# Encoder trunk on one core: the down product of the channel mixers by seven block products, half a part behind each gate and up unit of the next part

## The chip, the cores and the metric

The kernel runs on 1 core of one Trainium2 chip. The core has TensorE (PE, matrix products, with a separate weight load), VectorE (DVE), ScalarE (ACT), GpSimd (POOL) and SyncE (SP), which issues the DMA transfers here. Each engine works through its own queue in order and waits on semaphores of the others. The metric is the device time of one execution in microseconds (us), the median of several runs.

## What is computed

Two requests (512 and 256 tokens, 1024 features, fp32) go through two layers with the same weights. Each layer has a mixer over the sequence (a Fourier mixer first, a gated DeltaNet second) and then a channel mixer, and everything is scaled and shifted by a vector `c` (adaLN). The part that matters here is the channel mixer with its residual:

```python
def swiglu(h, w_gu, w_down):
    gu = h @ w_gu
    return (jax.nn.silu(gu[..., :FFN_DIM]) * gu[..., FFN_DIM:]) @ w_down
...
        mod = (cs @ ada_w[layer] + ada_b[layer])[:, None, :]
        sh1, sc1, g1, sh2, sc2, g2 = jnp.split(mod, 6, axis=-1)
...
        h = rmsnorm(x, norm_ffn_g[layer]) * (1.0 + sc2) + sh2
        x = x + g2 * swiglu(h, ffn_w_gu[layer], ffn_w_down[layer])
```

`FFN_DIM` is 2816, which is 22 chunks of 128.

## The kernel before

Features lie on the 128 partitions, the 768 tokens of both requests side by side in the columns. x is eight tiles `xs[m]` of 128 x 768. Every product is made in three passes: an operand is split into a rounded part (`wh`, `hh`, ...) by a cast on ACT and a remainder (`wl`, `hl`, ...) by a subtraction on DVE (`split_w`, L151 and L152, for weights; `split_to`, L199 and L200, for activations), and `passes` (L132 is the one matmul line of all helpers) adds high by high, high by low and low by high in one PSUM bank.

`gate_up` (from L375) computes gate and up of one chunk of 128 hidden features, or of two at the start. It takes the weights as a 2 x 2 block matrix (gate and up by the two halves of the inner dimension), the activations as a 2 x 2 block matrix (halves of the inner dimension by halves of the 768 tokens, `blocks`), and makes the product by seven block products (numbers 1, 2, 6, 7, 5, 4, 3, in that order) instead of eight. The weight combinations (`comb`, L379) are two on POOL and two on DVE. Below, such a pass over one chunk is called a unit; it has 7 products of 12 matmuls each.

`ffn` cuts the 22 chunks into the parts of `PARTS`. For each part it first makes all units and splits their results `sg` into `g` tiles; then, for each of the eight output rows m, `product` multiplies the part's rows of `ffn_w_down` by them, token columns 512 and 256 apart, and `residual` (L454, DVE) adds the gated result to `xs[m]`. In the second layer the last part goes to `finish`, which also normalizes and writes the output.

After each unit, and after each row of a down product, `between` advances the products of `c` with `ada_w` for later stages (`ada_steps`): fp32 matmuls that fill a quarter of PE's columns each (`sm<-at`, 4 to a step), with 256 KB transfers of their weights on SP into `AT1` = 4 buffers. This is done in the first layer alone; `AD` says how many steps go where.

The order on each engine isn't the program's text alone: the tile framework's scheduler lays the instructions of all engines out, and work marked `high_priority` (weight splits, combinations, copies out of PSUM) moves ahead. Weight tiles `wh` and `wl` have 5 buffers, fetched weights `stg` 4, `g` 10, and PSUM has 6 banks for `pr` in the first layer and 8 in the second.

Of the kernel before, what the change touches and what calls it, by code (L numbers as in the profile page):

```python
# [12 lines left out]
F32 = mybir.dt.float32  # L13
F32R = mybir.dt.float32r
AF = mybir.ActivationFunctionType
ALU = mybir.AluOpType
# [24 lines left out]
R2G = (3,)  # L41
# [68 lines left out]
def encoder_kernel(  # L110
# [264 lines left out]
    def gate_up(wgu, ms, blocks, psp, wk):  # L375

        def comb(eng, out, a, b, op):
            with tc.high_priority():
                eng.tensor_tensor(out, a, b, op)  # L379

        def parts(src):
            wh, wl = split_w(src)
            return [wh[:, k] for k in range(HK)], [wl[:, k] for k in range(HK)]

        def left(m):
            stg_g, stg_u = fetch(wgu, 0, KC, m * P), fetch(wgu, 0, KC, FFN + m * P)
            a11, a12, a21, a22 = stg_g[:, :HK], stg_g[:, HK:], stg_u[:, :HK], stg_u[:, HK:]
            yield parts(a11)
            yield parts(a12)
            s1 = wk.tile([P, HK, P], F32, name="s1", bufs=WS)  # L390
            comb(G, s1, a21, a22, ALU.add)
            comb(G, a21, a11, a21, ALU.subtract)
            comb(V, a11, s1, a11, ALU.subtract)
            yield parts(a11)
            yield parts(a21)
            yield parts(s1)
            yield parts(a22)
            comb(V, a12, a12, a11, ALU.subtract)
            yield parts(a12)

        def keep(dst, ps):
            with tc.high_priority():
                A_.copy(dst, ps[:, :HT])  # L403
# [23 lines left out]
        sg = [wk.tile([P, T], F32, name="sg", bufs=2) for _ in ms]  # L427
# [12 lines left out]

        def up2(i):
            keep(up[i][:, HT:], px[i])
            G.tensor_tensor(up[i][:, HT:], m7[i], up[i][:, HT:], ALU.add)  # L443

        step(((1, px, True, lambda i: keep(sg[i][:, :HT], px[i])), (2, pw, True, gate1)))
        step(((6, px, False, lambda i: keep(up[i][:, :HT], px[i])), (7, py, True, lambda i: keep(m7[i], py[i]))))
        step(((5, px, False, up2),
              (4, py, False, lambda i: V.tensor_tensor(up[i][:, :HT], py[i][:, :HT], up[i][:, :HT], ALU.add))))
        step(((3, px, False, gate2),))
        return sg, silu[-1]  # L450

    def residual(x, ps, gate, m):
        for g, (lo, ln) in enumerate(SEGS):
            V.scalar_tensor_tensor(x[:, lo : lo + ln], ps[g], modT[:, gate, m, g : g + 1], x[:, lo : lo + ln],  # L454
                                   ALU.mult, ALU.add)

    def ffn(l, blocks, xs, psp, wk, gt, between, last, done):

        for c0, cn in PARTS:
            gh, gl = [], []  # L460
            for ms in [(0, 1), *((m,) for m in range(2, cn))] if c0 == 0 else [(c0 + i,) for i in range(cn)]:
                sgs, silu = gate_up(ffn_w_gu[l], ms, blocks, psp, wk)
                for sg in sgs:
                    ah, al = gt.tile([P, T], F32R, name="g"), gt.tile([P, T], F32R, name="g")
                    split_to(ah, al, sg)
                    gh.append(ah)
                    gl.append(al)
                    between(AD[0])
            if c0 + cn == HC and last(c0, gh, gl, silu):
                return  # L470
            for m in range(KC):
                po = product(psp, load_block(ffn_w_down[l], c0, cn, m * P), gh, gl, cn)
                residual(xs[m], po, GATE[2 * l + 1], m)
                between(AD[1])
                if c0 + cn == HC:
                    done(m)


    xd = dram.tile([KC, P, T], F32, name="xd")
    with ExitStack() as l0:  # L480
# [114 lines left out]
        with ExitStack() as fs:  # L595
            apool = fs.enter_context(tc.tile_pool(name="apool1", reuse_waits="tile", bufs=AT1))
            wk = fs.enter_context(tc.tile_pool(name="wk0", reuse_waits="tile", bufs=1))
            gt = fs.enter_context(tc.tile_pool(name="gt0", reuse_waits="tile", bufs=10))
# [5 lines left out]
            ffn(0, blocks, xs, ppr, wk, gt, lambda n: advance(steps, n), lambda *_: ex.close(),  # L604
                lambda m: nc.sync.dma_start(xd[m], xs[m]))
            advance(steps)
            nk = ex.enter_context(tc.tile_pool(name="nk0", reuse_waits="tile", bufs=1))
            norm_h(2, xs, ppr, nk)
# [439 lines left out]
    with ExitStack() as l1:  # L1048
# [6 lines left out]
        gt = l1.enter_context(tc.tile_pool(name="gt1", reuse_waits="tile", bufs=10))  # L1055
# [114 lines left out]
```

## Time and profile before

| what | value |
| --- | --- |
| median of 3 runs | 1955.3 us (1954.84 to 1956.31) |
| the profiled execution, its time | 1951.27 us |
| its span in the trace | 1949.5 us |
| DVE busy over the span | 1242.4 us (64%) |
| ACT busy | 891.5 us (46%) |
| POOL busy | 403.8 us (21%) |
| mean granted TensorE clock | 0.988 |

The profile is of one execution. A row of its groups reads: line, engine, operation, tiles out<-in, shape, count, then busy time, mean ns of one, and the idle time of the engine just before them with what ended it. A matmul's duration there is longer than the distance to the next one, since matmuls are pipelined; the distance from start to start is what PE takes for it. The chain of work is followed back from the last instruction: at each step to what released it. Rows of the timeline give start, length, engine, line and tiles.

### The profile page before, as it was taken

The page shows a single profiled execution, that of the slowest core. Times are in us where ns is not written, and L with a number is a line of the kernel's source. Part 1 is how long each engine was busy: PE and PEld are TensorE (multiplying, and loading weights), DVE is VectorE, ACT ScalarE, POOL GpSimd, SP SyncE. Part 2 cuts the span into 40 slices and gives each one's busy share as a digit, 9 for nine tenths or more (in the row PEclk, how much of TensorE's full clock was granted, in tenths as well). Part 3 has the DMA queues.
Part 4 walks back from the last instruction along what each step waited for, and adds up shares of the span by engine and source line. Part 5 has one row for each costly group of instructions (what it writes and reads, how often), then busy time and mean ns, then how long its engine had stood idle before and what let it go on. Part 6 is the DMA issues. An engine that isn't in the chain of part 4 may idle for free.

```text
span 1949.5 us, 29608 instructions
## 1 busy us (share of the span) xinstructions
PE 1850.7 (95%) x11497; PEld 1635.5 (84%) x11497; DVE 1242.4 (64%) x2041; ACT 891.5 (46%) x1712; POOL 403.8 (21%) x346
## 2 busy tenths in 40 slices
PE   7898999999999998999999999999699999999998
PEld 6585988979898997878888788778489999999997
DVE  4637745546454557897787778763784655656565
ACT  3526523414233344756566656642563342524343
POOL 1314202112111200123213222320530211121231
PEclk9999999999999999999999999999899999999999
DMA  7653334353544133322221222142022222222211
GB/s 269 217 184 130 89 98 149 113 179 122 182 135 145 47 103 112 104 60 56 67 62 56 66 63 63 53 144 66 16 65 73 69 63 79 68 64 78 74 45 65
DMA packets 250661, 189.70 MB, mean 97 GB/s; under 512 B 20624, under 2 KB 219417, under 8 KB 250521
## 3 DMA queue, kind: packets, MB, share of 16 engines
q1 hardware_dynamic: 250112, 187.66, 31.9%
q8 instruction: 90, 1.47, 0.3%
q14 instruction: 50, 0.41, 0.1%
q10 hardware_dynamic: 409, 0.15, 0.0%
HBM read 174.36 MB, written 13.42 MB: 96 GB/s over the span
## 4 chain that ended last, share of the span: by engine, by line
PE 72%; DVE 12%; ACT 6%; DMA 5%; POOL 3%; issue 2%; SPq 0%; DVEq 0%; ACTq 0%; POOLq 0%
PE pr L132 62%; PE sm L132 8%; DVE wa L768 2%; DVE wl L152 1%; PE ax L132 1%; DMA at<-in_ada_w_dram 1%; DMA cc<-solved 1%; DVE g L349 1%; POOL yy L1013 1%; ACT wh L151 1%; DVE we L713 1%; DMA stg<-in_ffn_w_gu_dram 1%; PE big L132 1%; DVE tmp L885 1%; ACT we L714 1%
## 5 line engine op out<-in xcount | busy, mean ns | idle before, releaser
L151 ACT CAST wh<-stg 128x512 fp32r<-128x512 f32 (+1 forms) x468 | 278.7, 597 | 611.3 <-PE pr L132 569.2
L132 PE MATMUL pr<-hh,wh 128*128 128x384 f32 (+2 forms) x1488 | 512.8, 347 | 14.9 <-ACT sg L403 6.2
L132 PE MATMUL pr<-hl,wh 128*128 128x384 f32 (+2 forms) x1488 | 508.8, 342 | 6.4 <-DVE hl L200 5.3
L132 PE MATMUL pr<-hh,wl 128*128 128x384 f32 (+2 forms) x1488 | 507.7, 342 | 1.2 <-DVE wl L152 1.2
L152 DVE TENSOR_TENSOR wl<-stg,wh 128x512 fp32r<-128x512 f32 (+1 forms) x468 | 347.4, 744 | 227.4 <-ACT wh L151 217.7
L132 PE MATMUL pr<-g,wh 128*128 128x512 f32 (+1 forms) x1280 | 317.8, 339 | 0.0
L132 PEld LDWEIGHTS pr<-hh,wh 128*128 128x128 f32 x1488 | 281.4, 190 | 42.0 <-ACT sg L403 7.6
L132 PEld LDWEIGHTS pr<-hl,wh 128*128 128x128 f32 x1488 | 281.9, 189 | 24.1 <-DVE hl L200 7.7
L132 PEld LDWEIGHTS pr<-hh,wl 128*128 128x128 f32 x1488 | 281.6, 189 | 17.1 <-DVE wl L152 1.9
L132 PEld LDWEIGHTS pr<-g,wh 128*128 128x128 f32 x1280 | 217.3, 188 | 38.8 <-issue 5.8
L132 PE MATMUL pr<-g,wl 128*128 128x512 f32 (+1 forms) x640 | 215.3, 337 | 0.0
L132 PE MATMUL pr<-el,wh 128*128 128x384 f32 x528 | 180.5, 342 | 6.3 <-POOL el L200 5.8
L379 POOL TENSOR_TENSOR s<-stg 128x512 f32<-128x512 f32 x44 | 60.6, 1377 | 604.1 <-DMA stg<-in_ffn_w_gu_dram 498.8
L132 PE MATMUL pr<-eh,wh 128*128 128x384 f32 x528 | 180.6, 343 | 3.7 <-ACT eh L199 3.7
L132 PE MATMUL pr<-eh,wl 128*128 128x384 f32 x528 | 179.4, 340 | 0.0
L454 DVE SCALAR_TENSOR_TENSOR x<-pr,modT,x 128x512 f32<-128x512 f32 x96 | 58.9, 616 | 126.7 <-PE pr L132 126.3
L132 PEld LDWEIGHTS pr<-g,wl 128*128 128x128 f32 x640 | 120.2, 188 | 14.5
L768 DVE SCALAR_TENSOR_TENSOR wa<-pad,cwT,wa 128x770 f32<-128x770 f32 x96 | 109.9, 1145 | 4.8 <-ACT wa L765 3.6
L443 POOL TENSOR_TENSOR up<-m,up 128x384 f32<-128x384 f32 x44 | 52.5, 1192 | 282.1 <-ACT up L403 282.1
L132 PEld LDWEIGHTS pr<-eh,wh 128*128 128x128 f32 x528 | 100.2, 190 | 9.9 <-ACT eh L199 4.1
L132 PEld LDWEIGHTS pr<-el,wh 128*128 128x128 f32 x528 | 100.3, 190 | 8.9 <-POOL el L200 7.8
L132 PEld LDWEIGHTS pr<-eh,wl 128*128 128x128 f32 x528 | 100.3, 190 | 0.0
(343 smaller groups left out, 2686.0 us busy)
## 6 DMA issues: line engine op xcount, KB each, us to landing
stg<-in_ffn_w_gu_dram SPq DMA_DIRECT2D x88, 512.0 KB, 4.2
at<-in_ada_w_dram SPq DMA_DIRECT2D x112, 256.0 KB, 3.8
at<-in_ada_w_dram SPq DMA_DIRECT2D x40, 512.0 KB, 4.9
stg<-in_gdn_w_in_dram SPq DMA_DIRECT2D x33, 512.0 KB, 4.3
stg<-in_ffn_w_down_dram SPq DMA_DIRECT2D x48, 256.0 KB, 2.9
stg<-in_ffn_w_down_dram SPq DMA_DIRECT2D x32, 320.0 KB, 3.2
at<-in_final_ada_w_dram SPq DMA_DIRECT2D x32, 256.0 KB, 4.0
raw<-gcd SPq DMA_DIRECT2D x8, 768.0 KB, 4.0
```

Source lines behind the costliest of these rows:

```text
L132: return nc.tensor.matmul(out, lhsT, rhs, start=start, stop=stop, **kw)
L151: A_.copy(wh[:, :n], src)
L152: V.tensor_tensor(wl[:, :n], src, wh[:, :n].bitcast(F32), ALU.subtract)
L349: (G if m in YP else V).tensor_tensor(t, xs[m], rs, ALU.mult)
L379: eng.tensor_tensor(out, a, b, op)
L443: G.tensor_tensor(up[i][:, HT:], m7[i], up[i][:, HT:], ALU.add)
L454: V.scalar_tensor_tensor(x[:, lo : lo + ln], ps[g], modT[:, gate, m, g : g + 1], x[:, lo : lo + ln], ALU.mult, ALU.add)
L713: V.tensor_scalar(e, src, -44.0, None, ALU.max)
L714: A_.activation(e, e, AF.Exp, scale=-1.0)
L768: V.scalar_tensor_tensor(acc, pad[:, d : d + T + 2], wc[d], acc, ALU.mult, ALU.add)
L885: se.tensor_tensor(t, r4[:, :, : k + 1, k : k + 1].to_broadcast(sh), u4[:, :, k : k + 1, k + 1 :].to_broadcast(sh), ALU.mult)
L1013: G.tensor_tensor(so, so, sq, ALU.add)
```

## The change

The down product of a part of four chunks is made in two halves of four output rows each (`down4`, rows m0 to m0+3). The weights are a 2 x 2 block matrix (pairs of output rows by even and odd chunks), the right side too (even and odd chunks by the halves of the 768 tokens), and the product is made by seven block products in the same order as in `gate_up`. Each product has 12 matmuls: two rows, two inner chunks, three passes, 384 columns. Weights come as two 512 KB blocks. The first and third product's results go to x by ACT (scaled copy) and POOL (addition), the others by DVE in pieces of 384, or of 128 and 256 where the request changes. `right` makes the combinations of the `sg` tiles and their splits.

The order of the program changes too: a part's two halves are held back as `pending`, and one is made behind each of the first two units of the next part. Results `sg` of these units are split only when both halves are out. `PARTS` is now one list for each layer: in the first, five parts of four and a last one of two chunks, whose plain down product (`whole`) ends the layer; in the second, a first part of two (plain), then parts of four, the last of them as before in `finish`. The last part of the first layer has its `g` tiles in `hh` and `hl`. `AD` now gives 3 steps after each unit of the first part, 2 after later units, 4 after a half and 1 after a row of the last part. `sg` has 3 buffers instead of 2, `g` 14 instead of 10, and the pool `ext0` is closed after the layer, no longer before its last down product.

```diff
-PARTS = ((0, 5), (5, 5), (10, 4), (14, 4), (18, 4))
+PARTS = (((0, 4), (4, 4), (8, 4), (12, 4), (16, 4), (20, 2)), ((0, 2), (2, 4), (6, 4), (10, 4), (14, 4), (18, 4)))
...
-AD = (2, 2)
+AD = (3, 2, 4, 1)
...
+    def right(sgs, gt, first):
...
+        sa, sb = sgs
+        b2, t13, t42 = pair(), pair(), pair()
+        split_to(*b2, sb)
+        V.tensor_tensor(sa[:, HI], sb[:, HI], sa[:, HI], ALU.subtract)
+        V.tensor_tensor(sb[:, HI], sb[:, HI], sa[:, LO], ALU.subtract)
+        V.tensor_tensor(sb[:, LO], sb[:, LO], sb[:, HI], ALU.subtract)
+        split_to(*t42, sb)
+        split_to(*t13, sa)
...
+    def down4(l, c0, m0, rights, xs, psp, wk):
...
+            s1 = four(wk.tile([P, HK, P], F32, name="s1", bufs=WS))
+            comb(G, s1, a21, a22, ALU.add)
+            comb(G, a21, a11, a21, ALU.subtract)
+            comb(V, a11, s1, a11, ALU.subtract)
...
+            comb(V, a12, a12, a11, ALU.subtract)
...
+        pw, py, px = ([bank(psp) for _ in range(2)] for _ in range(3))
...
+        def high(row):
+            def fn(i, ps):
+                into(m0 + 2 * row + i, ps, HT, S0, 0)
+                into(m0 + 2 * row + i, ps, S0, T, 1)
+            return fn
+
+        def shared(row):
+            def fn(i, ps):
+                m = m0 + 2 * row + i
+                t = wk.tile([P, HT], F32, name="m7", bufs=M7)
+                with tc.high_priority():
+                    A_.activation(t, ps[:, :HT], AF.Copy, scale=modT[:, gate, m, 0:1])
+                G.tensor_tensor(xs[m][:, LO], xs[m][:, LO], t, ALU.add)
+            return fn
+
+        run(1, px, True, shared(0))
+        run(2, pw, True, low(0))
+        run(6, px, False, shared(1))
+        run(7, py, True, high(1))
+        run(5, px, False, high(1))
+        run(4, py, False, low(1))
+        run(3, px, False, high(0))
...
+            for ms in [(0, 1), *((m,) for m in range(2, cn))] if c0 == 0 else [(c0 + i,) for i in range(cn)]:
+                sgs, silu = gate_up(ffn_w_gu[l], ms, blocks, psp, wk)
+                held += zip(ms, sgs)
+                own = final and last is None and ms[-1] == HC - 1
+                if pending and not own:
+                    pending.pop(0)()
+                if not pending or own:
+                    for m, sg in held:
+                        take(m, sg)
+                    held = []
+                for _ in ms:
+                    between(AD[0] if c0 == 0 else AD[1])
...
+            pending = [partial(whole, c0, cn, gs)] if plain else [partial(half, c0, m0, gs) for m0 in (0, HK)]
```

How this moves instructions shows at three places. The first is PE in the first layer, around the products of `c`. Before, inside a down product (`pr<-g` are its matmuls, `sm<-at` those of `c`):

```order
L132 MATMUL pr<-g,wh 128x256 x2
L132 MATMUL pr<-g,wl 128x256
L132 MATMUL sm<-at,csT 32x256 x8
L132 MATMUL pr<-g,wh 128x512 x2
L132 MATMUL pr<-g,wl 128x512
```

Now, in the unit behind a half, 13 matmuls after a run of eight `sm<-at` (`hh` and `hl` are that unit's activations):

```order
L132 MATMUL pr<-hh_71,wh 128x384
L132 MATMUL sm<-at,csT 32x256 x2
L132 MATMUL pr<-hl_79,wh 128x384
L132 MATMUL sm<-at,csT 32x256 x2
L132 MATMUL pr<-hh_71,wl 128x384
L132 MATMUL pr<-hh_72,wh 128x384
L132 MATMUL pr<-hl_80,wh 128x384
L132 MATMUL pr<-hh_72,wl 128x384
L132 MATMUL pr<-hh_73,wh 128x384
L132 MATMUL sm<-at,csT 32x256 x2
L132 MATMUL pr<-hl_81,wh 128x384
```

Behind a half, two of its four steps stand in one run and two are spread over the next unit's matmuls in runs of two.

The second place is DVE in the second layer, in a down product. Before, between the rows of a part (`pad`, `qT`, `vT` are tiles of x, the numbered `pr` its PSUM banks):

```order
L454 SCALAR_TENSOR_TENSOR pad_12132<-pr_15776,modT_87,pad_12132 128x512
L454 SCALAR_TENSOR_TENSOR pad_12132<-pr_15789,modT_87,pad_12132 128x256
L152 TENSOR_TENSOR wl_15943<-stg_15940,wh_15942 128x512
L454 SCALAR_TENSOR_TENSOR qT_12133<-pr_15810,modT_87,qT_12133 128x512
L454 SCALAR_TENSOR_TENSOR qT_12133<-pr_15823,modT_87,qT_12133 128x256
L152 TENSOR_TENSOR wl_15977<-stg_15974,wh_15976 128x512
```

Now, in a part's first half, from the first weight split of the next unit on. Banks 16379 and 16380 are those of the fourth and sixth product, 16381 and 16382 those of the first, third, fifth and seventh:

```order
L152 TENSOR_TENSOR wl_16543<-stg_16538,wh_16542 128x512
L532 SCALAR_TENSOR_TENSOR vT_12446<-pr_16379,modT_87,vT_12446 128x128
L379 TENSOR_TENSOR stg_16538<-s1_16577,stg_16538 128x512
L532 SCALAR_TENSOR_TENSOR vT_12446<-pr_16379,modT_87,vT_12446 128x256
L532 SCALAR_TENSOR_TENSOR we_12447<-pr_16380,modT_87,we_12447 128x128
L152 TENSOR_TENSOR wl_16547<-stg_16538,wh_16546 128x512
L532 SCALAR_TENSOR_TENSOR we_12447<-pr_16380,modT_87,we_12447 128x256
L379 TENSOR_TENSOR stg_16538<-stg_16538 128x512
L532 SCALAR_TENSOR_TENSOR vT_12446<-pr_16381,modT_87,vT_12446 128x128
L152 TENSOR_TENSOR wl_16582<-stg_16538,wh_16581 128x512
L532 SCALAR_TENSOR_TENSOR vT_12446<-pr_16381,modT_87,vT_12446 128x256
```

An update of x that was two instructions in a row is now taken apart by a split or a combination of the next unit's weights.

The third place is the same stretch of a part's second half, where 16673 and 16674 are the banks of the fifth product:

```order
L379 TENSOR_TENSOR stg_16850<-stg_16850 128x512
L532 SCALAR_TENSOR_TENSOR wa_12450<-pr_16673,modT_87,wa_12450 128x128
L532 SCALAR_TENSOR_TENSOR wa_12450<-pr_16673,modT_87,wa_12450 128x256
L152 TENSOR_TENSOR wl_16894<-stg_16850,wh_16893 128x512
L532 SCALAR_TENSOR_TENSOR qT_13110<-pr_16674,modT_87,qT_13110 128x128
L532 SCALAR_TENSOR_TENSOR qT_13110<-pr_16674,modT_87,qT_13110 128x256
```

Here the split stands behind both updates of the first bank instead of between them.

More of the change, by code (lines that the diff above doesn't have):

```diff
@@ L455, in residual @@
                                    ALU.mult, ALU.add)
-    def ffn(l, blocks, xs, psp, wk, gt, between, last, done):
[L459 to L470, printed above, removed]
+    LO, HI = slice(0, HT), slice(HT, T)
@@ new lines, in right, with pair @@
+    def right(sgs, gt, first):
+        def pair():
+            return tuple(gt.tile([P, T], F32R, name="g") for _ in range(2))
+        sa, sb = sgs
[6 more added lines that the diff above has]
+        split_to(*t13, sa)
+        return {1: first, 2: [t[:, LO] for t in b2], 3: [t[:, HI] for t in b2], 5: [t[:, LO] for t in t13],
+                7: [t[:, HI] for t in t13], 4: [t[:, LO] for t in t42], 6: [t[:, HI] for t in t42]}
@@ new lines, in down4, with fetch2, four, comb @@
+    def down4(l, c0, m0, rights, xs, psp, wk):
+        w2d = ffn_w_down[l]
+        def fetch2(m):
+            stg = weights["stg"].tile([P, KC, P], F32, name="stg")
+            nc.sync.dma_start(stg.rearrange("p (k m) n -> p k (m n)", m=2),
+                              w2d[c0 * P : (c0 + 4) * P, m * P : (m + 2) * P].rearrange("(k p) n -> p k n", p=P))
+            return stg.rearrange("p (k m) n -> p k m n", m=2)
+        def four(t):
+            return t.rearrange("p (k m) n -> p k m n", m=2)
+        def comb(eng, out, a, b, op):
+            with tc.high_priority():
+                eng.tensor_tensor(out, a, b, op)
+        def parts(src):
+            wh, wl = (four(weights[name].tile([P, HK, P], F32R, name=name)) for name in ("wh", "wl"))
+            with tc.high_priority():
+                A_.copy(wh, src)
+                V.tensor_tensor(wl, src, wh.bitcast(F32), ALU.subtract)
+            return wh, wl
+        def left():
+            s_a, s_b = fetch2(m0), fetch2(m0 + 2)
+            a11, a12, a21, a22 = s_a[:, 0::2], s_a[:, 1::2], s_b[:, 0::2], s_b[:, 1::2]
+            yield parts(a11)
+            yield parts(a12)
+            s1 = four(wk.tile([P, HK, P], F32, name="s1", bufs=WS))
+            comb(G, s1, a21, a22, ALU.add)
+            comb(G, a21, a11, a21, ALU.subtract)
+            comb(V, a11, s1, a11, ALU.subtract)
+            yield parts(a11)
+            yield parts(a21)
+            yield parts(s1)
+            yield parts(a22)
+            comb(V, a12, a12, a11, ALU.subtract)
+            yield parts(a12)
+        lefts = left()
+        pw, py, px = ([bank(psp) for _ in range(2)] for _ in range(3))
+        gate = GATE[2 * l + 1]
+        def run(n, ps, first, then):
+            wh, wl = next(lefts)
+            for i in range(2):
+                for _ in passes(ps[i][:, :HT], ([wh[:, k, i] for k in range(2)], [wl[:, k, i] for k in range(2)]),
+                                [r[n][0] for r in rights], [r[n][1] for r in rights], first, skip_group_check=True):
+                    pass
+                then(i, ps[i])
+        def into(m, ps, a, b, g):
+            x = xs[m][:, a:b]
+            o = HT if a >= HT else 0
+            V.scalar_tensor_tensor(x, ps[:, a - o : b - o], modT[:, gate, m, g : g + 1], x, ALU.mult, ALU.add)
+        def low(row):
+            return lambda i, ps: into(m0 + 2 * row + i, ps, 0, HT, 0)
+        def high(row):
[7 more added lines that the diff above has]
+                t = wk.tile([P, HT], F32, name="m7", bufs=M7)
+                with tc.high_priority():
+                    A_.activation(t, ps[:, :HT], AF.Copy, scale=modT[:, gate, m, 0:1])
[8 more added lines that the diff above has]
+        run(3, px, False, high(0))
@@ L473, in ffn, with half, pair, take @@
                 residual(xs[m], po, GATE[2 * l + 1], m)
-                between(AD[1])
                 if c0 + cn == HC:
+                    between(AD[3])
                     done(m)
+        def half(c0, m0, gs):
+            down4(l, c0, m0, gs, xs, psp, wk)
+            between(AD[2])
+        def pair():
+            return tuple(gt.tile([P, T], F32R, name="g") for _ in range(2))
+        pending, held = [], []
+        for c0, cn in PARTS[l]:
+            final = c0 + cn == HC
+            plain = cn < 4 or (final and last is not None)
+            gs, firsts = [], []
+            def take(m, sg):
+                if plain:
+                    gs.append((hh[m - HC], hl[m - HC]) if final and last is None else pair())
+                    split_to(*gs[-1], sg)
+                elif (m - c0) % 2 == 0:
+                    if m == c0:
+                        firsts.append(pair())
+                    h = [t[:, HI if m - c0 == 2 else LO] for t in firsts[0]]
+                    split_to(*h, sg[:, LO])
+                    V.tensor_tensor(sg[:, LO], sg[:, HI], sg[:, LO], ALU.subtract)
+                    firsts.append((sg, h))
+                else:
+                    sa, h = firsts[-1]
+                    gs.append(right((sa, sg), gt, h))
+            for ms in [(0, 1), *((m,) for m in range(2, cn))] if c0 == 0 else [(c0 + i,) for i in range(cn)]:
[10 more added lines that the diff above has]
+                    between(AD[0] if c0 == 0 else AD[1])
+            if final and last is not None:
+                last(c0, *zip(*gs), silu)
+                return
+            for fn in pending:
+                fn()
+            pending = [partial(whole, c0, cn, gs)] if plain else [partial(half, c0, m0, gs) for m0 in (0, HK)]
+        for fn in pending:
+            fn()
     xd = dram.tile([KC, P, T], F32, name="xd")
@@ L603, in encoder_kernel @@
             steps = ada((5, 7, 6, 8, 10, 9, 11, 13, 12), psm, apool, 2)
-            ffn(0, blocks, xs, ppr, wk, gt, lambda n: advance(steps, n), lambda *_: ex.close(),
+            ffn(0, blocks, xs, ppr, wk, gt, lambda n: advance(steps, n), None,
                 lambda m: nc.sync.dma_start(xd[m], xs[m]))
+            ex.close()
             advance(steps)
```

8 lines of the change are left out of this document (5 added, 3 removed).

## Prediction

> **What bounds the kernel now.** I read the page first, then the busy time of each engine in stretches of the two channel mixers (the SwiGLU layers; the two stretches shown lie one in each), then the chain of work there, then the timeline and the groups of instructions of the engines that feed TensorE (PE).
>
> ```profile
> span 1949.5 us, 29608 instructions
> ...
> 500.00:600.00 100.00, 99.59 (x638) 85.93 (x637) 51.57 (x81) 32.01 (x58) 14.56 (x11) 1.00 0.48 149
> ...
> 1600.00:1750.00 150.00, 150.00 (x861) 139.81 (x860) 84.29 (x125) 51.13 (x95) 25.41 (x20) 1.00 0.24 70
> ```
>
> The columns of the two lower rows are the stretch, its length, then PE, weight load, VectorE (DVE), ScalarE (ACT) and GpSimd (POOL) busy, granted clock, DMA share, GB/s. PE is busy for all of it at full clock; DVE for 52 to 56%. In the mixers time is PE time, so an instruction taken off PE counts in full as long as PE doesn't begin to wait.
>
> ```profile
> 432.64 5.25 PE pr L132 x30
> 469.43 1.00 PE sm L132 x16
> 470.43 14.77 PE pr L132 x84
> 530.15 4.20 PE pr L132 x24
> 577.84 14.56 PE pr L132 x84
> 1447.07 434.35 PE pr L132 x2487
> ```
>
> These are pieces of the chain: start, length, count. 84 matmuls are the gate and up product of one chunk (already seven block products); where nothing stands between, they take 14.56 us. 24 and 30 are the down product of one output row for a part of 4 or 5 chunks: 4.20 and 5.25 us, so 1.05 us for a chunk and row. In the second mixer 2487 matmuls run 434.35 us without any other engine on the chain.
>
> **The halves: what PE saves.** Four output rows of a four-chunk part cost 4 x 4.20 = 16.80 us now. The new half does them in 7 products x 2 inner chunks x 2 rows x 3 passes = 84 matmuls of 384 columns, the form and number of a gate and up unit: 14.56 us. That is 2.24 us less. There are 5 such parts in the first mixer and 4 in the second, two halves each: 18 x 2.24 = 40.3 us. The parts of 2 chunks stay plain, at the same price per chunk. Bounds: the 84 matmuls have the same shapes as those measured, so 39 to 41.
>
> **The modulation product, cut in pieces.** In the first mixer PE also does the conditioning vector's matmuls (sm<-at), in steps that `between` places. The work is the same, 88 of 90 steps fall before the last part. But the order of the changed kernel breaks it: behind the opening units, for the same 235 matmuls, the program before has 28 runs of 8 and one each of 7, 3 and 1, the changed one 17 of 8, one of 7 and 46 of 2, each run between `pr` matmuls.
>
> ```profile
> 561.34 0.34 PE L132 MATMUL pr<-hl,wh 128*128 128x384 f32 x1
> 561.52 0.34 PE L132 MATMUL pr<-hh,wl 128*128 128x384 f32 x1
> 561.79 1.07 PE L132 MATMUL sm<-at,csT 128*32 128x256 f32 x16
> 562.79 0.45 PE L132 MATMUL pr<-eh,wh 128*128 128x384 f32 x1
> 563.07 0.34 PE L132 MATMUL pr<-el,wh 128*128 128x384 f32 x1
> ...
> 504.53 0.28 PE L132 MATMUL pr<-g,wh 128*128 128x256 f32 x1
> 504.74 0.62 PE L132 MATMUL sm<-at,csT 128*32 128x256 f32 x2
> 505.29 0.51 PE L132 MATMUL pr<-g,wh 128*128 128x512 f32 x1
> 505.63 0.39 PE L132 MATMUL pr<-g,wl 128*128 128x512 f32 x1
> ```
>
> A run of 8 shows as 16 records. `pr` matmuls start 0.175 us apart; here 0.27 passes before the run, 1.00 inside, 0.28 from the first `pr` behind it to the next. So a run of 8 costs 1.20 us. The lone run (2 records) still takes 0.55 us to the next `pr`, and the same two edges: 0.75 us. Four runs of 2 cost 3.0 us where one of 8 costs 1.2. Before: 28 x 1.20 + 1.2 + 2 x 0.75 = 36.3; after: 17 x 1.20 + 1.2 + 46 x 0.755 = 56.3; **+20.0 us**. Lower bound: the edges cost nothing at a run of 2 (46 x 0.55), +10.6.
>
> ```profile
> L132 PEld LDWEIGHTS sm<-at,csT 128*32 128x32 f32 x470 | 13.4, 108 | 16.1 <-DMA at<-in_ada_w_dram 4.3 <-DMA at<-in_final_ada_w_dram 2.4 <-issue 1.8
> ...
> at<-in_ada_w_dram SPq DMA_DIRECT2D x112, 256.0 KB, 3.8
> ```
>
> The first row says that such runs now wait 4.3 + 2.4 = 6.7 us for their DMA. After, the first run of 2 stands 13 `pr` matmuls behind a run of 8 that frees its buffers: PE is there about 3.4 us after that run began, while a transfer issued some 0.2 to 0.6 us into it needs 3.8. I take 0.5 us for each of nine places, 4.5 in all (9 if each is 1 us): -2.2 against now. Net for this part +17.8, bounds 8.4 and 22.3.
>
> **What the halves ask of DVE.** Here the change adds waits. Seven products share six PSUM banks; the sixth adds into the bank of the fourth and the seventh into the bank of the fifth, so PE may not start them before DVE has put the earlier value into x. The DVE queue has weight splits and combinations of the next unit between these updates, so a late split holds the update behind it, and PE waits for that update.
>
> ```profile
> L152 DVE TENSOR_TENSOR wl<-stg,wh 128x512 fp32r<-128x512 f32 x132 | 102.1, 774 | 64.7 <-ACT wh L151 59.7 <-PE pr L132 3.6
> L151 ACT CAST wh<-stg 128x512 fp32r<-128x512 f32 x131 | 81.4, 621 | 161.5 <-PE pr L132 148.0 <-issue 10.8 <-POOL up L443 2.5
> L379 POOL TENSOR_TENSOR stg<-stg 128x512 f32<-128x512 f32 x18 | 28.1, 1559 | 1.4
> L379 POOL TENSOR_TENSOR s<-stg 128x512 f32<-128x512 f32 x18 | 25.5, 1418 | 239.8 <-DMA stg<-in_ffn_w_gu_dram 184.2 <-DVE stg L379 36.7 <-DVE wl L152 18.9
> L443 POOL TENSOR_TENSOR up<-m,up 128x384 f32<-128x384 f32 x20 | 23.3, 1165 | 125.0 <-ACT up L403 125.0
> L454 DVE SCALAR_TENSOR_TENSOR wa<-pr,modT,wa 128x512 f32<-128x512 f32 x8 | 6.0, 751 | 10.9 <-PE pr L132 10.9
> L454 DVE SCALAR_TENSOR_TENSOR wa<-pr,modT,wa 128x256 f32<-128x256 f32 x8 | 3.8, 480 | 2.5 <-PE pr L132 2.5
> ```
>
> ```profile
> 1633.67 0.42 DVE L152 TENSOR_TENSOR wl<-stg,wh 128x256 fp32r<-128x256 f32 x1 [0.63 <-ACT wh L151]
> ...
> 1639.44 1.63 POOL L379 TENSOR_TENSOR stg<-stg 128x512 f32<-128x512 f32 x1
> 1639.83 0.47 DVE L454 SCALAR_TENSOR_TENSOR wa<-pr,modT,wa 128x256 f32<-128x256 f32 x1
> 1640.22 1.39 DVE L379 TENSOR_TENSOR stg<-stg 128x512 f32<-128x512 f32 x1
> ...
> 1644.47 0.69 DVE L152 TENSOR_TENSOR wl<-stg,wh 128x512 fp32r<-128x512 f32 x1 [0.97 <-PE pr L132]
> 1645.08 0.48 DVE L454 SCALAR_TENSOR_TENSOR qT<-pr,modT,qT 128x256 f32<-128x256 f32 x1
> 1645.48 0.68 DVE L152 TENSOR_TENSOR wl<-s,wh 128x512 fp32r<-128x512 f32 x1
> ```
>
> From start to start a split takes 0.61 and a 256-wide update 0.40; between 480 and 751 ns the update grows by 1.06 ns a column, so a 384-wide one is 0.53 and a 128-wide one 0.27. A half gives DVE 7 splits, 2 combinations, 4 updates of 384 and 6 pairs of 128 and 256: 9 x 0.61 + 4 x 0.53 + 6 x 0.67 = 11.6 us of 14.56. It fits, but not everywhere. Take the end of the third product as zero; the seventh may start at 3 x 2.08 = 6.24. Until then DVE must do, in the order of a first half, 3 splits, 2 combinations, 3 narrow and 3 wide updates: 5 x 0.61 + 3 x 0.27 + 3 x 0.40 = 5.06, behind a cast of 0.62 and about 0.3 (a matmul shows 0.34 us at 0.175 between starts, so a product's end is seen 0.17 late, and the last update's write takes 0.08 more): 5.98. Slack 0.26. Yet POOL is at work too: one of the new additions into x (as L443, 1.17 us) and the two combinations of the unit after next, which start when its weights land, in this stretch. Beside POOL the combination of 1640.22 took 1.39 instead of 0.69, and the mean split 0.77. Three rows lie under POOL's work here; with about 0.35 each, 1.05 us, PE waits **0.8 us** in each first half. In second halves the third split stands behind the update, which gives 0.61 more room; there the second row's bank comes late instead, I take 0.25. 9 x 0.8 + 9 x 0.25 = 9.5 us. Bounds a half: nothing (no row slowed) and 1.9 (three rows doubled, 2.07, and slack gone).
>
> The Trainium skill, page SBUF — State Buffer, section "SBUF: two separate sides", says that VectorE with two SBUF inputs and GpSimd share a port pair under an exclusive lock, so that the later one blocks fully. By it every row of the three would double: 1.9 us in every half, 34 us, and by the sum below 1968 us. The trace agrees for one row, at 1.39 us, but not for the mean of 132, 0.77.
>
> ACT gets 7 casts of 0.62 and 4 reads of a 384-wide bank, which are narrower than a cast: under 6.9 us a half, so room. The new splits of g (right) fall into gate and up units, where DVE has half its time free. SP fetches two 512 KB blocks a half instead of four of 256 KB: hidden, since their buffers come free two units ahead; without that cover each would cost PE at least the 3.8 us that 256 KB need to land.
>
> **The end of the first mixer.** The last part has 2 chunks, so a row takes PE 2.1 us; DVE per row does updates, a split of 256 and a sum of squares of 768.
>
> ```profile
> 737.97 0.96 DVE L300 TENSOR_TENSOR sq<-sq 128x768 f32<-128x768 f32 x1 [0.97 <-ACT sq L296]
> 739.32 0.75 DVE L454 SCALAR_TENSOR_TENSOR x<-pr,modT,x 128x512 f32<-128x512 f32 x1 [0.39 <-PE pr L132]
> ```
>
> That is 0.66 + 0.40 + 0.34 + 0.88 = 2.28 (0.08 off each, as above): it ends up to 8 x 0.18 us late. +1.5, bounds 0 and 3.
>
> **Sum.** -40.3 + 17.8 + 9.5 + 1.5 = -11.5 us. The profiled execution took 1951.3 us (span 1949.5), which gives 1939.8; the median of the runs, 1955.3, lies 4.0 above, so **1944 us**, 0.6% less.
>
> **Rivals.**
> - Halves without waits (0.22): 9.5 falls away, 1934 us; with the pieces of the modulation at their lower bound too, 1925. For it: DVE has 3 us to spare in a half, and the splits run up to five buffers ahead of PE. Against: the slack at the seventh product is 0.26.
> - DVE sets the pace (0.15): the seventh product waits for x in every half because splits, combinations and POOL's additions hold each other up. From (40.3 - 17.8 - 1.5) / 18 = 1.17 us a half on it eats the gain; at 1.7 us it costs 30.6, so 1965 us, and at the bound of 1.9 it is 1968. For it: POOL has 7.6 us of work a half (4 x 1.17 + 1.42 + 1.56). Against: updates that read PSUM keep their time beside POOL (0.47 at 1639.83).
> - A wash (0.16): waits of 0.95 to 1.38 us a half, 1951.4 to 1959.2 us; the same mechanism, half as strong.
> - That the halves do no less work is excluded: their 84 matmuls stand in the order.
>
> The forecast has 0.47, from 1936 to 1951. A time within 0.2% of before (1951.4 to 1959.2 us) is about what can't be told from no change; less is faster, more slower: 0.69, 0.16, 0.15. The range that leaves out two in ten, half at each end, is 1927 to 1963.
>
> **What would show it.** Right: chain pieces of 84 matmuls in 14.6 us for the halves; a `pr` bank released by DVE (the update of x, L532) as what PE waits for at the start of the seventh product, under 1 us; many short `sm` pieces of 0.55 us. Wrong: PE waits of over 1.2 us a half; pieces of 2 at 0.3 us; waits for casts or splits of `g`; a mixer stage whose PE time isn't 84 x 0.175.

## The result and the profile after

| | before | changed |
| --- | --- | --- |
| median of 20 runs | 1956.0 us | 1961.5 us |
| the profiled execution's span | 1949.5 us | 1959.8 us |
| DVE busy over the span | 64% | 75% |
| POOL busy | 21% | 29% |

The ratio is 1.0026, 95% interval 1.0017 to 1.0036: slower by about a quarter of a per cent, just clear of noise. The forecast was 1944 us; the time lies within the range, on the side to which the forecast gave 0.15.

From the page of the changed kernel the first row, and from its busy time by stretches the two stretches shown for the kernel before (length, then PE, weight load, DVE, ACT and POOL busy, granted clock, DMA share, GB/s):

```profile
span 1959.8 us, 30027 instructions
...
500.00:600.00 100.00, 97.18 (x574) 83.09 (x574) 72.42 (x111) 41.76 (x75) 31.46 (x23) 1.00 0.40 125
1600.00:1750.00 150.00, 145.75 (x829) 143.91 (x828) 129.43 (x184) 74.60 (x136) 56.15 (x39) 1.00 0.23 70
```

PE, which was busy for all of either stretch, now idles for 2.8 and 4.2 us of them. DVE went from 52 and 56% to 72 and 86%, POOL's work doubled. What PE waits for stands in the view of waits of the changed kernel (who waits for whom: us in total, times, longest), first for the first mixer, then for the second from its second part on:

```profile
PE pr L132 <- DVE x L532: 13.3, 14, 1.9
...
PE pr L132 <- DVE vT L532: 6.2, 4, 1.7
PE pr L132 <- DVE qT L532: 2.0, 4, 0.9
PE pr L132 <- DVE wa L532: 1.9, 3, 0.7
```

Apart from 0.9 us for the DMA of the conditioning weights, all of it is the update of x in a half, L532. The view counts idle time; counted as start-to-start distances above 0.175 us within each half, the 18 halves lose 34.6 us, 1.92 each: 1.6 to 2.1 us at the start of the seventh product in every first half, and in second halves several smaller waits from the sixth product on (1.9 to 2.8 us together; the last half of each layer loses 0.1 and 0.6). Not all of the 34.6 is waiting. At the end of the half that starts at 359.3 us PE is busy but its granted clock (the column behind POOL's) is low:

```profile
375.00:378.00 3.00, 3.00 (x15) 2.74 (x17) 1.71 (x4) 0.52 (x1) 0.00 (x0) 0.57 0.00 0
```

Nine matmuls start 0.32 us apart there instead of 0.175. That is about 1.3 us, so some 33.3 us are waits, 1.85 a half.

By landmarks in the two traces, us from start to start (the first mixer from the first matmul of its first unit to the last matmul of its down product, then the norm behind it, then the whole sequence mixer, then the second channel mixer to the end):

| stretch | before | changed | difference |
| --- | --- | --- | --- |
| to the first unit | 164.9 | 164.9 | +0.1 |
| first channel mixer | 575.5 | 585.9 | +10.4 |
| to the next mixer's first matmul | 7.9 | 11.0 | +3.1 |
| sequence mixer | 645.7 | 648.0 | +2.3 |
| second channel mixer and finish | 551.7 | 546.3 | -5.4 |

### The profile page after: what moved, and what is told of

The parts are those of the page before. It is cut to its first block, busy times and chain, and to the rows that moved or that the text cites. A ratio compares the mean times of both kernels' runs of the same rounds, so it can differ in the third digit from the quotient of the medians.

```text
span 1959.8 us, 30027 instructions
## 1 busy us (share of the span) xinstructions
PE 1842.1 (94%) x11281; PEld 1636.7 (84%) x11281; DVE 1468.8 (75%) x2399; ACT 977.8 (50%) x1858; POOL 563.7 (29%) x454
## 4 chain that ended last, share of the span: by engine, by line
PE 69%; DVE 14%; ACT 6%; DMA 5%; issue 3%; POOL 3%; ACTq 0%; SPq 0%; DVEq 0%; POOLq 0%
PE pr L132 58%; PE sm L132 8%; DVE wl L152 3%; DVE wa L913 2%; DMA at<-in_ada_w_dram 1%; PE ax L132 1%; DMA cc<-solved 1%; ACT wh L151 1%; POOL yy L1158 1%; DVE we L858 1%; PE big L132 1%; DVE x L532 1%; DVE tmp L1030 1%; ACT we L859 1%; DMA at<-in_final_ada_w_dram 1%
## 5 line engine op out<-in xcount | busy, mean ns | idle before, releaser
L132 PE MATMUL pr<-hl,wh 128*128 128x384 f32 (+2 forms) x1520 | 522.8, 344 | 5.2 <-DVE hl L200 4.2
L132 PE MATMUL pr<-hh,wl 128*128 128x384 f32 (+2 forms) x1520 | 520.7, 343 | 1.2 <-DVE wl L152 1.2
L151 ACT CAST wh<-stg 128x512 fp32r<-128x512 f32 (+1 forms) x380 | 230.7, 609 | 394.7 <-PE pr L132 324.3
L152 DVE TENSOR_TENSOR wl<-stg,wh 128x512 fp32r<-128x512 f32 (+1 forms) x380 | 315.2, 832 | 127.7 <-ACT wh L151 124.7
L132 PE MATMUL pr<-g,wh 128*128 128x384 f32 (+2 forms) x1072 | 278.3, 341 | 23.6 <-DVE x L532 13.3
L132 PEld LDWEIGHTS pr<-g,wh 128*128 128x128 f32 x1072 | 191.8, 188 | 37.0 <-DVE x L532 19.8
L379 POOL TENSOR_TENSOR s<-stg 128x512 f32<-128x512 f32 x44 | 62.6, 1423 | 453.4 <-DMA stg<-in_ffn_w_gu_dram 362.7
L132 PE MATMUL pr<-g,wl 128*128 128x384 f32 (+2 forms) x536 | 181.1, 338 | 0.0
L498 DVE TENSOR_TENSOR wl<-stg,wh 128x512 fp32r<-128x512 f32 x108 | 99.8, 924 | 36.0 <-ACT wh L497 33.8
L497 ACT CAST wh<-stg 128x512 fp32r<-128x512 f32 x108 | 67.1, 621 | 81.5 <-PE pr L132 67.1
L132 PEld LDWEIGHTS pr<-g,wl 128*128 128x128 f32 x536 | 101.0, 188 | 0.7
```

The source lines that it names most:

```text
L132: return nc.tensor.matmul(out, lhsT, rhs, start=start, stop=stop, **kw)
L151: A_.copy(wh[:, :n], src)
L152: V.tensor_tensor(wl[:, :n], src, wh[:, :n].bitcast(F32), ALU.subtract)
L497: A_.copy(wh, src)
L498: V.tensor_tensor(wl, src, wh.bitcast(F32), ALU.subtract)
```

## The experiments

Nine kernels were run, one of them twice. Their times are compared as ratios to the kernel before, run on the same chip (its median was 1951.9 to 1956.4 us from call to call).

**The updates first.** One line of the changed kernel:

```diff
-            V.scalar_tensor_tensor(x, ps[:, a - o : b - o], modT[:, gate, m, g : g + 1], x, ALU.mult, ALU.add)
+            with tc.high_priority(): V.scalar_tensor_tensor(x, ps[:, a - o : b - o], modT[:, gate, m, g : g + 1], x, ALU.mult, ALU.add)
```

> The changed kernel with one line altered: the VectorE updates of x in the halves are marked high priority, so that they stand in the queue ahead of the next unit's second combination and third split instead of behind them. Profiled, the changed kernel's PE waits 34 us in 18 halves (1.9 us each), 1.6 to 2.05 us of it at the start of the seventh product of a first half. Theory A (the weight rows ahead of the updates, lengthened beside GpSimd, make the update late): the waits at the seventh product nearly go, below 0.5 us a half, so 20 to 28 us less than the changed kernel, 1934 to 1941 us. Rival B (VectorE lacks time in a half as a whole, whatever the order): the wait moves to the next unit's weights, PE waits as long for wl, and the time stays at 1958 to 1964 us.

Measured 1931.9 us, ratio 0.9891 (0.9876 to 0.9906): 26 us less than the changed kernel by the ratios. The waits in the 18 halves are 0.3 us in all. Theory A holds and rival B falls. Below, DVE in the timeline of a first half of the changed kernel, with POOL and PE at the same place:

```profile
1645.69 1.11 POOL L549 TENSOR_TENSOR we<-we,m 128x384 f32<-128x384 f32 x1 [0.31 <-ACT m L548]
1646.11 1.24 DVE L379 TENSOR_TENSOR stg<-s,stg 128x512 f32<-128x512 f32 x1
...
1648.31 1.47 POOL L492 TENSOR_TENSOR s<-stg 128x512 f32<-128x512 f32 x1 [1.50 <-DMA stg<-in_ffn_w_down_dram]
1648.53 0.47 DVE L532 SCALAR_TENSOR_TENSOR we<-pr,modT,we 128x256 f32<-128x256 f32 x1
1648.92 1.40 DVE L379 TENSOR_TENSOR stg<-stg 128x512 f32<-128x512 f32 x1
1649.86 1.61 POOL L492 TENSOR_TENSOR stg<-stg 128x512 f32<-128x512 f32 x1
1650.25 0.34 DVE L532 SCALAR_TENSOR_TENSOR vT<-pr,modT,vT 128x128 f32<-128x128 f32 x1
1650.51 1.50 DVE L152 TENSOR_TENSOR wl<-stg,wh 128x512 fp32r<-128x512 f32 x1
1650.61 0.33 PE L132 MATMUL pr<-g,wl 128*128 128x384 f32 x1
1651.94 0.47 DVE L532 SCALAR_TENSOR_TENSOR vT<-pr,modT,vT 128x256 f32<-128x256 f32 x1
1652.46 0.61 PE L132 MATMUL pr<-g,wh 128*128 128x384 f32 x2 [1.53 <-DVE vT L532]
```

The last PE row is the seventh product; it waits for the update that ends at 1652.41. Ahead of that update stand three rows that read both inputs from SBUF and take 0.69 us when alone: 1.24, 1.40 and 1.50. Together they grew by 2.08 us, and PE is late by 1.68 (1652.46 less 1650.61 less 0.175). The first two end 0.55 us after the POOL instruction that was running when they started (1647.35 against 1646.80; 1650.32 against 1649.78), and the third too (1652.01 against 1651.47). The updates, which read PSUM, keep 0.34 and 0.47 beside POOL.

The same place with the updates first:

```profile
1624.38 0.73 DVE L532 SCALAR_TENSOR_TENSOR vT<-pr,modT,vT 128x128 f32<-128x128 f32 x2
1625.03 0.85 DVE L379 TENSOR_TENSOR stg<-s,stg 128x512 f32<-128x512 f32 x1
1625.81 0.73 DVE L532 SCALAR_TENSOR_TENSOR we<-pr,modT,we 128x128 f32<-128x128 f32 x2
1626.46 0.73 DVE L532 SCALAR_TENSOR_TENSOR vT<-pr,modT,vT 128x128 f32<-128x128 f32 x2
1627.11 1.18 DVE L152 TENSOR_TENSOR wl<-stg,wh 128x512 fp32r<-128x512 f32 x1
1628.21 0.73 DVE L532 SCALAR_TENSOR_TENSOR we<-pr,modT,we 128x128 f32<-128x128 f32 x2
1628.86 1.13 DVE L379 TENSOR_TENSOR stg<-stg 128x512 f32<-128x512 f32 x1
```

Both pieces of an update now stand together, and the update of the fifth product (1626.46) ahead of the split and the second combination. Rows beside POOL are still longer (1.18, 1.13), but nobody waits for them. The chain of this kernel has a piece of PE alone through two halves:

```profile
1499.93 79.95 PE pr L132 x457
```

Something was given back. By the landmarks the second mixer is 8.0 us shorter than in the changed kernel, though some 14 us of waits are gone from its halves: three of its units wait 0.4 to 0.7 us for ACT's copy of their third product out of PSUM (1.7 us in all; in the first of them the copy stands behind a cast of g); where the other 4 to 5 us went was not traced.

**POOL quiet.** In the halves, and the second piece also in the units:

```diff
-                G.tensor_tensor(xs[m][:, LO], xs[m][:, LO], t, ALU.add)
...
-            comb(G, s1, a21, a22, ALU.add)
-            comb(G, a21, a11, a21, ALU.subtract)
-            comb(V, a11, s1, a11, ALU.subtract)
+            comb(V, a11, a22, a11, ALU.subtract)
...
-            yield parts(s1)
+            yield parts(a22)
```

> The changed kernel without the additions of GpSimd into x and without GpSimd's two weight combinations of each unit and half (the third combination uses a22 in place of their sum; both are left out in the channel mixers of both layers). VectorE's rows in the halves and their order stay as they are. Theory A1 (VectorE's SBUF rows are lengthened by GpSimd, and that makes PE wait): with GpSimd quiet the splits take 0.69 us and combinations 0.68 all through, the waits fall from 1.9 to at most 0.4 us a half, the time by 27 to 33 us to 1928 to 1935 us. Rival A2 (the order of the queue alone is too late, contention adds little): waits of over 1.2 us a half stay, 1950 us or more.

This kernel leaves out POOL's additions into x and its two weight combinations; the third combination takes a22 instead of their sum. Measured 1921.6 us, ratio 0.9839 (0.9824 to 0.9854), some 37 us below the changed kernel, more than expected; the waits in the halves are 0.1 us in all, and the sequence mixer, which the edit doesn't touch, was 3.9 us shorter in the profiled execution. The same rows in its timeline, in the same order:

```profile
1615.01 0.68 DVE L379 TENSOR_TENSOR stg<-stg 128x512 f32<-128x512 f32 x1
...
1617.26 0.68 DVE L379 TENSOR_TENSOR stg<-stg 128x512 f32<-128x512 f32 x1
1617.86 0.34 DVE L526 SCALAR_TENSOR_TENSOR vT<-pr,modT,vT 128x128 f32<-128x128 f32 x1
1618.34 0.69 DVE L152 TENSOR_TENSOR wl<-stg,wh 128x512 fp32r<-128x512 f32 x1
1618.94 0.48 DVE L526 SCALAR_TENSOR_TENSOR vT<-pr,modT,vT 128x256 f32<-128x256 f32 x1
```

DVE even idles before the split (from 1618.20 to 1618.34). So the bad order alone costs PE nothing in the halves, and lengthened rows alone (the run before) cost nothing there: the wait needs both.

**Half of POOL's work.** Two kernels: one leaves out the additions into x, one the two combinations (edits as above, one at a time).

> The changed kernel without GpSimd's additions into x in the halves (left out: the first and third product's shares of x); GpSimd's combinations stay. In the profiled first half of 1638 us, the rows that grew ahead of the late update are one combination by 0.55 us beside an addition, and a combination by 0.71 and a split by 0.82 beside GpSimd's two combinations. If each growth counts in full: first halves wait 1.1 to 1.3 us instead of 1.7 to 1.9. In second halves, two of four grown rows (0.72 and 0.82) lie beside additions and come early, so the waits at the sixth product go and those at the seventh stay: 0.5 to 1.0 in place of 1.8. Time 14 to 22 us below the changed kernel. If the additions are all of it: below 0.3 us a half; if nothing: 1.9.

Measured 1936.9 us, ratio 0.9901 (0.9885 to 0.9917), 24 us below the changed kernel, a little more than expected. First halves wait 1.07 us in the mean (0.5 to 1.45), just below what was expected; second halves not at all (0.01), where 0.5 to 1.0 was expected. So their waits at the seventh product hang on the additions too, most likely as a late start inherited from the sixth.

> The changed kernel without GpSimd's two combinations of each unit and half (the third combination uses a22 in their place; left out in both mixers); the additions into x stay. By the same rows: first halves lose 1.53 of their growth and wait at most 0.4 us; second halves keep the waits at the sixth product (0.2 to 1.0 us) and lose some of those at the seventh, 0.5 to 1.2 us in all. Time 20 to 28 us below the changed kernel. If combinations don't matter: 1.9 us a half as in the changed kernel.

Measured 1926.4 us, ratio 0.9846 (0.983 to 0.9863), 35 us below, more than expected. First halves wait 0.26 us, second ones 0.67, both as expected. So first halves owe their wait mostly to POOL's combinations, second halves need the additions: without them none is left, without the combinations a third. The waits account for 26 us of the 35, and 4.1 us come from the sequence mixer between the channel mixers, which was that much shorter in this execution (643.9 us against 648.0; it lay between 643.9 and 648.1 in all twelve traces, whatever the edit). The other 5 us were not traced.

**The conditioning steps inside the half.** `half` no longer calls `between(AD[2])`; `down4` does:

```diff
-        run(1, px, True, shared(0))
+        run(1, px, True, shared(0)); between(AD[2] // 2)
...
-        run(7, py, True, high(1))
+        run(7, py, True, high(1)); between(AD[2] // 2)
```

> The changed kernel with the four steps of the conditioning products behind each half moved into the half, two behind its first product and two behind its fourth. In PE's order the runs of 2 go from 47 to 5 and the runs of 8 from 18 to 29. If the pieces cost what the changed kernel's trace shows against that of before (13 us more for the same matmuls), the time falls by 10 to 14 us, to 1948 to 1952 us; if the pieces are hidden or the cost was DMA waits, by less than 4 us, 1957 us or more. The waits for VectorE in the halves stay at 1.9 us each.

Measured 1926.3 us, ratio 0.9866 (0.9853 to 0.988): 31 us below the changed kernel, more than twice what was expected. The runs of `sm<-at` give some 19 us of it. Counted from the start of each run to the next `pr`, plus what the `pr` matmuls at both edges take above their usual distance (once, where one `pr` stands between two runs), they cost 43.0 us before, 57.3 in the changed kernel and 38.3 here; a run of 8 costs 1.20 us in the median, a run of 2 0.76. But the waits of the first mixer went as well. The view of waits for the first mixer has, instead of 13.3 us:

```profile
PE pr L132 <- DVE x L532: 2.2, 3, 0.9
```

and the timeline of PE shows why:

```profile
492.74 0.34 PE L132 MATMUL pr<-g,wl 128*128 128x384 f32 x1
493.01 1.07 PE L132 MATMUL sm<-at,csT 128*32 128x256 f32 x16
494.01 0.61 PE L132 MATMUL pr<-g,wh 128*128 128x384 f32 x2
```

A run of 8, work that PE must do anyway, now stands between the fourth and the fifth product, which gives DVE 1.2 us more ahead of the seventh. In the second mixer, which has no such runs, the waits stayed (5.5, 2.4 and 1.6 us for the three x tiles).

**One layer alone.** The first mixer as before (`ffn_old` is `ffn` of the kernel before, with its parts, steps and buffers), the second as changed; then the same with the updates first.

```diff
-            ffn(0, blocks, xs, ppr, wk, gt, lambda n: advance(steps, n), None,
+            ffn_old(0, blocks, xs, ppr, wk, gt, lambda n: advance(steps, n), lambda *_: ex.close(),
                 lambda m: nc.sync.dma_start(xd[m], xs[m]))
-            ex.close()
```

> The first channel mixer as in the kernel before (parts of 5, 5, 4, 4, 4, plain down products, steps of the conditioning products as before), the second as in the changed kernel. By the traces the second mixer gained 4.5 us on PE (16.8 less product time, 14.2 us of waits, 2 us less in units) and the first lost 10 there and 3 in its tail, so 1950 to 1953 us, 3 to 6 below before. If instead the second mixer gave nothing and the difference between the two traces lay elsewhere (the stretch between the mixers was 2 us longer in the changed one), 1955 to 1958 us.

Measured 1948.0 us, ratio 0.9978 (0.9966 to 0.999), 3.9 us below the kernel before on that chip (by the interval 2 to 7), near the 5.4 of the landmarks.

> First mixer as in the kernel before, second as in the changed kernel with the updates of x at high priority. In the trace of the second mixer with the updates ahead the waits are 0.15 us in 8 halves, against 15.4 where they are not. So 13 to 16 us below the kernel with the second mixer changed alone (1948.0), 1932 to 1935 us, and 17 to 20 us below before (8 x 2.24 = 17.9): the whole of the saving, in a mixer without conditioning products.

Measured 1937.7 us beside a before of 1956.4, ratio 0.9907 (0.9892 to 0.9922): 18.7 us below before (by the interval 15 to 21). Where hardly anything waits (0.7 us in eight halves), this agrees with the 8 x 2.24 = 17.9 us that the prediction counted; by the landmarks the second mixer is 15.6 us shorter than before.

**Both edits.** The updates first and the steps inside the half.

> The changed kernel with both edits: the updates of x at high priority, and the four steps of the conditioning products inside each half. If the two terms are separate (pieces about 17 us, waits about 34 us), the time would fall by 51 us, to about 1906 us. But with the steps inside the halves, the runs of 8 between the fourth and fifth product already gave VectorE 1.2 us in each half of the first mixer, whose waits fell to 4.9 us in all, so what is left to gain there is 4.9, and 14.9 us in the second mixer: 1907 to 1914 us, 12 to 20 below the kernel with the steps inside alone. Above 1918 us one of the two undoes the other.

Measured 1907.5 us, ratio 0.9753 (0.9738 to 0.9767), and 1908.8 us, 0.9762 (0.9742 to 0.9782), when run again. It beats both kernels, 2.4% below before, and by the ratios it is 22 us below the kernel with the steps inside alone, a little over the 12 to 20 expected. The two edits nearly add up: 26 and 31 us alone, 53 together.

> The same kernel as both_edits, beside the one above on the same chip: 2.3 to 2.6% below before; the stretch from the last down matmul of the first mixer to the first matmul of the next mixer 10 to 12 us.

**The end of the first mixer.** Chain of waits of the changed kernel from the last down matmuls to the next norm (start, length, what):

```profile
744.78 6.33 PE pr L132 x36
...
751.70 1.89 DVE wl L152 x3
753.59 0.40 DVE x L454
753.98 0.88 DVE sq L300
754.86 0.04 issue
754.90 3.80 PE pr L132 x4
```

Four weight splits of the next mixer stand on DVE ahead of the last update, and the last sum of squares behind it, on which all eight matmuls with `ones` wait: PE idles 3.8 us, from 751.1 to 754.9. Before, that sum stood ahead of the splits, so four of the eight ran right behind the down product. The last row of the chain shows something else: four of these matmuls take 3.80 us, where before they start 0.43 us apart. From the view by stretches, first the changed kernel while they run, then the kernel below:

```profile
754.90:760.30 5.40, 5.31 (x8) 2.52 (x8) 0.20 (x1) 2.67 (x5) 0.00 (x0) 0.54 1.07 357
...
708.00:712.00 4.00, 2.62 (x11) 1.45 (x11) 3.98 (x7) 2.45 (x5) 0.00 (x0) 1.00 0.55 210
```

The granted clock was 0.54. Of the 3.1 us by which the stretch grew, PE's idle time is only 0.65 (4.8 us before, 5.4 now); the rest is the slower matmuls. In the eight traces in which PE waits 3.8 us or more at this place, the granted clock falls to 0.5 during that wait or within 0.8 us of its end; in the four others it falls only after the next mixer has begun. On top of both edits:

```diff
-                residual(xs[m], po, GATE[2 * l + 1], m)
+                if c0 + cn == HC:
+                    with tc.high_priority(): residual(xs[m], po, GATE[2 * l + 1], m)
+                else: residual(xs[m], po, GATE[2 * l + 1], m)
...
-                V.tensor_tensor(parts[-1], parts[-1], sq, ALU.add)
+                with tc.high_priority() if tail else ExitStack(): V.tensor_tensor(parts[-1], parts[-1], sq, ALU.add)
```

> The kernel with both edits, and at the end of the first mixer the last part's updates of x and the sums of squares at high priority, so that on VectorE three of the next mixer's four weight splits (2.49 us for four) stand behind the last sum instead of ahead of it. In the changed kernel PE goes 10.9 us from the last matmul of the down product to the first of the next mixer, in the one before 7.8. If the late sums of squares are the cause, the stretch gets shorter by 1.5 to 2.5 us and with it the time, by about 0.1%, which only the trace can show; if the splits are then late for PE themselves, nothing changes there.

Measured 1905.2 us, ratio 0.9744 (0.9725 to 0.9763), not to be told from both edits by the time. The stretch from the last down matmul to the first of the next mixer is 7.6 us, against 11.3 in the kernel beside it and 7.9 before, a larger step than the 1.5 to 2.5 us expected. PE's first wait there is 1.0 us, and the clock stays at 1.00. In the timeline the sum has gone ahead of the splits:

```profile
708.69 0.95 DVE L300 TENSOR_TENSOR sq<-sq 128x768 f32<-128x768 f32 x1
709.55 0.68 DVE L152 TENSOR_TENSOR wl<-stg,wh 128x512 fp32r<-128x512 f32 x1
710.16 0.48 DVE L454 SCALAR_TENSOR_TENSOR x<-pr,modT,x 128x256 f32<-128x256 f32 x1
710.55 1.88 DVE L152 TENSOR_TENSOR wl<-stg,wh 128x512 fp32r<-128x512 f32 x3
```

## Why the prediction was wrong, step by step

**Right: what PE saves.** A half takes 14.56 to 14.99 us in the kernel with the updates first, against 14.56 counted, and the second mixer alone gave 18.7 us by the medians (15.6 by the landmarks) for 17.9 counted.

**Right, but too large: the pieces of the modulation product.** +17.8 was forecast, 43.0 to 57.3 = +14.3 measured, inside the bounds. The run of 2 was priced at 0.75 and cost 0.76; the 4.5 us of DMA waits that the sum allowed for hardly came (0.9 us in the view of waits).

**Wrong: what the halves ask of DVE.** 9.5 us was forecast and 33.3 us of waits came, 1.85 a half, next to the upper bound of 1.9. That alone turns the forecast gain into a loss. The mechanism was right, and for first halves the place too (the seventh product waits for the update of x); two sizes were not.

- For first halves the step was "Three rows lie under POOL's work here; with about 0.35 each, 1.05 us". In the half shown they cost 0.55, 0.71 and 0.82, 2.08 us in all; less the slack of 0.26 that is 1.8, and first halves lost 1.6 to 2.1. The prediction doesn't work the 0.35 out. It lies between the 0.70 by which one combination grew and the 0.08 of the mean of 132 splits, and that mean averages rows with nothing on POOL beside them and rows that do have it. The number to use stood in the prediction's own fence: the combination of 1640.22 that took 1.39, and ends at 1641.61, 0.54 us after the POOL row that was running (1639.44 plus 1.63). In the channel mixers of the kernel before, 58 of the 128 x 512 weight splits and combinations start beside a running POOL instruction, and 55 of them end 0.54 to 0.56 us after it; in those of the changed kernel it is 164 of 176. The others start within 0.15 us of that instruction's start or end. A row's end there is set by the rest of POOL's instruction, not by a share of it.
- For second halves the step was "there the second row's bank comes late instead, I take 0.25", with the new splits of g falling "into gate and up units". The first of `take`'s and `right`'s rows (L595, L469) fall into the second half itself, beside the additions, and 1.9 to 2.8 us are lost from the sixth product on. Timeline of the changed kernel's second half:

```profile
1675.50 0.54 DVE L595 TENSOR_TENSOR sg<-sg 128x384 f32<-128x384 f32 x1
1675.58 1.34 POOL L549 TENSOR_TENSOR wa<-wa,m 128x384 f32<-128x384 f32 x1 [1.55 <-ACT m L548]
1676.08 1.26 DVE L469 TENSOR_TENSOR sg<-sg 128x384 f32<-128x384 f32 x1
1676.92 1.30 POOL L549 TENSOR_TENSOR qT<-qT,m 128x384 f32<-128x384 f32 x1
1677.26 1.50 DVE L152 TENSOR_TENSOR wl<-stg,wh 128x512 fp32r<-128x512 f32 x1
1678.69 0.34 DVE L532 SCALAR_TENSOR_TENSOR wa<-pr,modT,wa 128x128 f32<-128x128 f32 x1
```

L595 started first and kept its 0.54; the two rows that started beside a running addition took 1.26 and 1.50, and the update behind them starts only when the second has ended. That the waits of second halves come from the additions is shown by the kernel without them: 0.01 us are left.

The Trainium skill, page SBUF — State Buffer, section "SBUF: two separate sides", says that of a VectorE row with two SBUF inputs and a GpSimd row the one that starts first holds the ports for the whole instruction and the other fully blocks. The prediction weighed that rule, found it in one row and set it aside because the mean of 132 rows didn't show it. The trace agrees with it in nearly every row: those that started first kept 0.54 us (L595, 384 wide) or 0.69 (512 wide), those that started second ended behind the POOL row (0.55 us behind at 512 wide, 0.42 for L469 at 384). By the rule the prediction had 34 us of waits; 33.3 were measured. That the two sums are so near is in part luck: the prediction put the same 1.9 us into every half, while second halves lost up to 2.8 by other rows, and the last half of each layer 0.1 and 0.6.

**The rivals.** "DVE sets the pace" is what happened, with its chance of 0.15 too low: at 1.9 us a half it gave 1968. Of the 6.5 us between that and the median, 4.0 are what the sum had added for the profiled execution of before, faster than its runs (1951.3 against a median of 1955.3); the profiled execution of the changed kernel was as long as its median. The other 2.5 are what is left of terms that partly cancel: the pieces cost 3.5 us less than summed and the waits in the first units of both mixers got 3.9 us shorter; the end of the first mixer cost 1.6 more and the sequence mixer took 2.3 longer. That DVE has time in a half as a whole, which spoke against this rival, is true, as the updates-first kernel shows, and did not help: it is the row ahead that counts, not the total.

**Too small: the end of the first mixer.** +1.5 was forecast, bounds 0 and 3, and 3.1 came. The estimate took a row's lag of 0.18 us eight times; the splits of the next mixer ahead of the last sum were not counted, nor the granted clock of 0.54 behind the long wait, which is most of the 3.1. With the sum ahead of the splits all 3.1 us went, the low clock with them. That the long wait brings the low clock is likely by the twelve traces, but no kernel changed one without the other.

**Not forecast:** the sequence mixer, +2.3 us, has the same instructions in nearly the same order and varies by more between the traces (643.9 to 648.1 us).

**Left open.** With the updates first, some 6 us were given back in the second mixer, 1.7 of them in waits for ACT's copies; no kernel tried to take that away. Why the clock fell in one half out of 18 is open too.

## What to carry to other kernels

Price a row by the company it will have where it is put, from the rows that already have such company, and not by the mean of its group: here 1.2 to 1.5 us in the rows that made PE wait, instead of 0.77. Where PE waits for a PSUM bank to be read, put the reads ahead of the weight work for later products in the same queue; one line did that, and was worth 26 us. And put filler work for PE in whole runs at the places where it waits for another engine anyway: the same matmuls cost 19 us less and hid most of a mixer's waits. A wait of several us can also cost more than its length: here eight matmuls behind one ran at a granted clock of 0.54.

## What was not expected of the hardware

DVE rows of 128 x 512 with both inputs in SBUF took 0.69 us alone and 1.31 in the median beside POOL: of 176 that started beside a running POOL instruction in the channel mixers of the changed kernel, four in five ended between 0.547 and 0.552 us after the end of that instruction. Updates that read PSUM kept their time (0.34 and 0.47 us) there. A POOL instruction that starts while such a DVE row runs is longer in its turn: POOL's second combination of L379 took 1.62 us in the median instead of 1.29.
